# A two-layer hybrid decoder step: second chunk's input in its own stream, GpSimd's two-input work moved

## The chip, the cores and the metric

The kernel runs on one core of a Trainium2 chip. The core has TensorE (PE in the profile), VectorE (DVE), ScalarE (ACT), GpSimd (POOL) and SyncE (SP, here only an issuer of DMAs). The metric is the device time of one execution in microseconds, lower is better; the time of the kernel before is the median of three runs.

## The reference

One inference step of a two-layer decoder over 512 prompt tokens and 8 sample sequences of 8 new tokens each, model width 1024, all in float32. Per layer:

```
h = rmsnorm(x, norm_mix_g)
u, z, xbc, dt, cq, ckv, kpe = split(h @ w_in)            # 1702 columns
pool = windows 2/4/8/16 of u, minus u, times pool_w
ssd  = Mamba-2 scan over silu(causal conv4(xbc)), gated by silu(z), rmsnorm
mla  = 6 heads on a compressed latent: q = rmsnorm(cq) @ w_uq, rotary part,
       scores against rmsnorm(ckv) and rope(kpe), softmax, values, rmsnorm
x = x + concat(pool, ssd, mla) @ w_out
x = x + square(relu(rmsnorm(x) @ w_up)) @ w_down         # 4096 hidden
```

The sample sequences also read a paged cache of 1024 past positions (a page table picks the pages), and past pool, conv and scan states. After the layers comes one last rmsnorm; the new states, latents and rope keys are outputs too.

## The kernel before

Activations lie transposed: 128 features in the partitions, tokens along the free axis. The tokens are two chunks: chunk 0 is prompt tokens 0 to 255, chunk 1 is prompt tokens 256 to 511 and the 64 sample tokens (320 wide). Every matmul with big weights is done in three passes on rounded halves (`gemm`, L196): high weights by high activations, high by low, low by high (the lines L201 to L203 of the profile). `wblock` (L183) loads 128 x 512 pieces of a weight on the SP queue, rounds each on ScalarE (L191) and makes the low half by a subtraction (L192): on VectorE for w_up and w_down, and for w_in, w_out and w_uq on GpSimd for the first piece of a block and on VectorE for the second. A block of eight k tiles is 24 matmuls.

The work of one layer and chunk is a set of generators made by `mixer` (L348): `w_in` (14 blocks of the input projection, each evacuated by `evac`, L460), `mla_proj`, `prompt_attn`, `sample_attn` (chunk 1 alone), `ssd_dt`/`ssd`/`ssd_out`, `pool_out`, `mla_out` and `w_out`. They wait for each other by names (`need`, `mark`). `Weave` (L272) writes them down in turns: it always advances the generator whose sum of yielded costs, divided by its rate, is smallest; a generator that waits yields None. A scheduler then orders the instructions of each engine from that order of writing, with shifts of priority (`tc.high_priority`, `tc.cur_priority`). On an engine the instructions then run strictly in that order. Weights are written 100 steps ahead, evacuations of w_in 500, the scan and prompt attention 1000.

`start` (L328) loads the input of chunk 0 in eight pieces and prepares it with `prep0` (L238): for each of eight k tiles a scaled high half on ScalarE and a low half on VectorE (`scaled_split`, L234), and the squares for the first RMS norm. The odd tiles are squared on ScalarE and added up on VectorE, the even ones are squared and added on GpSimd (L247 to L251); `rstd_of` (L210) sums the two over the partitions by matmuls with ones. Then the same is written for chunk 1 (L340 to L345), with the priority counter moved 400 steps later for this part.

The first stage writes the mixer of layer 0, chunk 0, then w_out of chunk 0 at rate 1.0 beside the mixer of chunk 1, until w_out is done and the input projection of chunk 1 is written (L1089 to L1096). After it the feed-forward part of chunk 0 (`ffn`, L995) goes beside attention of chunk 1; 64 steps of 24 matmuls each. `late` (L999) names the step after which w_out of the next mixer may start: 40 beside chunk 0, 24 beside chunk 1. Layer 1 repeats this: the mixer of chunk 0 (its attention beside the feed-forward part of layer 0, chunk 1), then chunk 1.

A convolution tile (`conv_tile`, L387) is: product with rstd into XB on VectorE, copies of the halo on GpSimd (L391, L398), one tensor-scalar and three scalar-tensor-tensor steps on VectorE (L400, L402), a sigmoid of three ScalarE steps, and the gating product (L405, L407) on GpSimd. XB has one buffer. GpSimd also has the gate of z (L479), the rope residue of each cache piece (L671), the scaling of the probabilities (L581, L698), the windows of the pool (L436) and the scan state of the samples (L886, L890).

`prompt_attn` (L558) goes through three pairs of heads; for each head and each block of 128 queries: scores, row maximum (L576) and its negation (L577) on VectorE, exponential with its sum on ScalarE, reciprocal, scaling on GpSimd, transposes on PE, evacuation into pT (two buffers, a tag that the sample attention shares), and products with the values (L591) into one half of the partitions of `po`.

## Time and profile before

| what | value |
|---|---|
| median of 3 runs | 1501.34 us (1498.47 to 1504.32) |
| profiled execution | 1500.04 us |
| its span | 1498.2 us |
| PE busy | 1418.7 us (95%) |
| VectorE busy | 1067.8 us (71%) |
| ScalarE busy | 816.9 us (55%) |
| GpSimd busy | 341.5 us (23%) |
| granted TensorE clock, mean | 0.98 |

Busy times are sums over an engine's instructions in the one profiled execution. A busy PE is not PE at its peak, since matmuls overlap and their ends are modelled; the stages differ, so the table by stages among the rows below is read before the totals.

### The profile page before, as it was taken

Reading aid. Unit: us, or ns where it says so; the run is one execution under the profiler, and the core shown is the slowest. Engines: PE = TensorE matmul, PEld = TensorE weight load, DVE = VectorE, ACT = ScalarE, POOL = GpSimd, SP = SyncE. Lnnn points to the kernel's source line nnn. Section 1 sums busy time; section 2 is a strip of 40 time slices with the busy share of each in tenths; the row PEclk is TensorE's granted clock in tenths of the full one; section 3 lists DMA queues with packets and bytes.
Section 4 is the critical chain, followed back from the end, with each engine's and each line's share of the span. In section 5 each row is a group of like instructions: output and inputs, shape, how many; then the busy total and the mean of one; then the engine's idle time right before and its main releaser. Section 6 shows DMA issues by size and latency. Waiting matters only on the chain.

```text
span 1498.2 us, 30372 instructions
## 1 busy us (share of the span) xinstructions
PE 1418.7 (95%) x10528; PEld 1355.6 (90%) x10528; DVE 1067.8 (71%) x2225; ACT 816.9 (55%) x1717; POOL 341.5 (23%) x458
## 2 busy tenths in 40 slices
PE   5988988999999979999999999999999999999997
PEld 4867977998999978999999998889989999999997
DVE  7878759776666779865566668976866667765765
ACT  6555636555565656655454556545656565443444
POOL 5456424222200235200100035511231011000000
PEclk8999999999999999999999999989999999999999
DMA  6322425667546634434554543455675455444443
GB/s 215 108 96 77 146 70 172 201 201 211 154 138 186 199 106 135 149 104 149 163 153 153 168 153 111 149 169 165 197 225 158 135 174 165 152 150 149 149 152 108
DMA packets 151995, 228.96 MB, mean 153 GB/s; under 512 B 17826, under 2 KB 60962, under 8 KB 151714
## 3 DMA queue, kind: packets, MB, share of 16 engines
q1 hardware_dynamic: 138178, 216.69, 46.3%
q10 hardware_dynamic: 13664, 10.34, 2.3%
q8 instruction: 83, 1.36, 0.4%
q14 instruction: 70, 0.57, 0.1%
HBM read 219.32 MB, written 7.64 MB: 151 GB/s over the span
## 4 chain that ended last, share of the span: by engine, by line
PE 81%; DVE 11%; issue 2%; DMA 2%; ACT 2%; SPq 1%; POOL 0%; ACTq 0%; DVEq 0%; POOLq 0%
PE dn L203 9%; PE dn L201 9%; PE dn L202 9%; PE up L203 9%; PE up L201 9%; PE up L202 9%; PE in L203 2%; PE in L202 2%; PE in L201 2%; PE out L201 2%; PE out L202 2%; PE out L203 2%; PE o L591 2%; DVE cv L402 2%; PE spo L717 1%
## 5 line engine op out<-in xcount | busy, mean ns | idle before, releaser
L201 PE MATMUL up<-gh_f,wh_up 128*128 128x256 f32 (+1 forms) x1024 | 308.7, 302 | 5.0 <-DVE UE L425 2.6
L203 PE MATMUL up<-gh_f,wl_up 128*128 128x256 f32 (+1 forms) x1024 | 307.2, 301 | 3.4 <-DVE wl_up L192 1.9
L202 PE MATMUL up<-gl_f,wh_up 128*128 128x256 f32 (+1 forms) x1024 | 306.9, 300 | 0.7 <-DVE gl_f L236 0.5
L201 PE MATMUL dn<-hh,wh_dn 128*128 128x256 f32 (+1 forms) x1024 | 303.8, 297 | 3.3 <-ACT wh_dn L191 3.2
L203 PE MATMUL dn<-hh,wl_dn 128*128 128x256 f32 (+1 forms) x1024 | 304.2, 297 | 0.0
L202 PE MATMUL dn<-hl,wh_dn 128*128 128x256 f32 (+1 forms) x1024 | 303.3, 297 | 0.0
L191 ACT ACTIVATE wh_dn<-wr_dn 128x512 fp32r<-128x512 f32 x256 | 160.9, 631 | 184.6 <-PE dn L202 126.1
L191 ACT ACTIVATE wh_up<-wr_up 128x512 fp32r<-128x512 f32 x256 | 160.3, 630 | 172.4 <-PE up L202 107.4
L192 DVE TENSOR_TENSOR wl_dn<-wr_dn,wh_dn 128x512 fp32r<-128x512 f32 x256 | 179.2, 701 | 84.1 <-ACT wh_dn L191 72.6
L192 DVE TENSOR_TENSOR wl_up<-wr_up,wh_up 128x512 fp32r<-128x512 f32 x256 | 182.2, 715 | 73.6 <-ACT wh_up L191 63.3
L201 PEld LDWEIGHTS up<-gh_f,wh_up 128*128 128x128 f32 x1024 | 195.4, 191 | 9.0 <-DVE UE L425 2.8
L203 PEld LDWEIGHTS up<-gh_f,wl_up 128*128 128x128 f32 x1024 | 195.2, 191 | 6.8 <-DVE wl_up L192 4.6
L202 PEld LDWEIGHTS up<-gl_f,wh_up 128*128 128x128 f32 x1024 | 195.7, 191 | 2.6 <-DVE gl_f L236 0.8
L201 PEld LDWEIGHTS dn<-hh,wh_dn 128*128 128x128 f32 x1024 | 193.3, 189 | 3.9 <-ACT wh_dn L191 3.7
L203 PEld LDWEIGHTS dn<-hh,wl_dn 128*128 128x128 f32 x1024 | 193.2, 189 | 1.4 <-issue 0.7
L202 PEld LDWEIGHTS dn<-hl,wh_dn 128*128 128x128 f32 x1024 | 193.3, 189 | 1.2 <-issue 0.9
L201 PE MATMUL in<-gh_h,wh_in 128*128 128x256 f32 (+3 forms) x448 | 137.9, 308 | 16.2 <-DVE cq L490 7.5
L203 PE MATMUL in<-gh_h,wl_in 128*128 128x256 f32 (+3 forms) x448 | 137.6, 307 | 3.5 <-DVE wl_in L192 2.4
L202 PE MATMUL in<-gl_h,wh_in 128*128 128x256 f32 (+3 forms) x448 | 137.2, 306 | 2.1 <-DVE gl_h L236 2.1
L192 POOL TENSOR_TENSOR wl_in<-wr_in,wh_in 128x512 fp32r<-128x512 f32 (+1 forms) x55 | 72.9, 1326 | 155.8 <-ACT wh_in L191 149.8
L192 POOL TENSOR_TENSOR wl_out<-wr_out,wh_out 128x512 fp32r<-128x512 f32 x32 | 41.8, 1306 | 278.7 <-ACT wh_out L191 278.7
L201 PEld LDWEIGHTS in<-gh_h,wh_in 128*128 128x128 f32 (+1 forms) x448 | 85.1, 190 | 18.9 <-issue 7.9
(349 smaller groups left out, 2849.4 us busy)
## 6 DMA issues: line engine op xcount, KB each, us to landing
wr_up<-in_w_up SPq DMA_DIRECT2D x256, 256.0 KB, 2.8
wr_dn<-in_w_down SPq DMA_DIRECT2D x256, 256.0 KB, 2.8
wr_in<-in_w_in SPq DMA_DIRECT2D x110, 256.0 KB, 2.8
wr_out<-in_w_out SPq DMA_DIRECT2D x64, 256.0 KB, 2.9
ku<-in_kcache SPq DMA_DIRECT2D x96, 128.0 KB, 2.9
nat<-in_ncache SPq DMA_DIRECT2D x96, 64.0 KB, 2.0
ku<-in_kcache ACTq DMA_DIRECT2D x32, 128.0 KB, 3.7
wr_uq<-in_w_uq SPq DMA_DIRECT2D x12, 256.0 KB, 2.8
```

What stands on the lines that cost most here:

```text
L191: A.activation(hh, r, AF.Copy)
L192: (V if eng == 'v' or (f and eng is None) else G).tensor_tensor(ll, r, hh.bitcast(F32), op=ALU.subtract)
L201: T.matmul(ps[:mw, :cw], wh[:, kk, :mw], ah, start=(k == 0), stop=False)
L202: T.matmul(ps[:mw, :cw], wh[:, kk, :mw], al, start=False, stop=False)
L203: T.matmul(ps[:mw, :cw], wl[:, kk, :mw], ah, start=False, stop=(k == nk - 1))
L402: V.scalar_tensor_tensor(cv[:, :n], X[:, k:k + n], par(l, 'conv_w', m * 4 + k), cv[:, :n], op0=ALU.mult, op1=ALU.add)
L591: mark_pe[f"pa{l}{c}"] = T.matmul(po[64 * hh:64 * hh + 64, b * P:b * P + P], vT[i // 2][:, i % 2, h * 64:h * 64 + 64], pT[:, i * P:i * P + ...
L717: mark_pe[f"s{l}{2 * pq_ + 1}"] = T.matmul(po[:, 64 * u:64 * u + NR], nat[:, g], pT[:, o_:o_ + NR], start=False, stop=True, skip_group_che ...
```

## The change

- The chunk-1 input is no longer written in `start` but by a generator `prep1` in the weave, at rate 0.8, from the fourth block of w_in on; it loads in four pieces.
- `prep0` squares all eight tiles on ScalarE. For chunk 0 each square is added up by a matmul with ones as it comes; for chunk 1 the squares overwrite the input and `rstd_of` adds eight of them with matmuls.
- w_out of chunk 0 in layer 0 is written at rate 2.0; before it the weave runs until the chunk-1 input is prepared.
- `late` is 28 instead of 40 beside chunk 0.
- Gating products, rope residues and all low weight halves are on VectorE; the probabilities are scaled on ScalarE.
- In `prompt_attn` both heads of a pair are transposed before their value products, which alternate between the heads.
- The row maximum is negated in the reduction itself.

```
--- before.py
+++ after.py
@@ -90,7 +90,7 @@
 def step_kernel(ctx: ExitStack, tc: tile.TileContext, I, O):
     nc = tc.nc
     V, A, G, T, S = nc.vector, nc.scalar, nc.gpsimd, nc.tensor, nc.sync
-    E_XA, E_Z, E_KR, E_PR = G, G, G, G
+    E_XA, E_Z, E_KR = V, V, V
 
     const = ctx.enter_context(tc.tile_pool(name="const", bufs=1))
     wp = ctx.enter_context(tc.tile_pool(name="wp", bufs=2))
@@ -189,7 +189,7 @@
                 lo = wp.tile([P, HB, P], F32R, tag="wl", name=f"wl_{name}_{f}", bufs=NWL)
                 r, hh, ll = raw[:, :, :mw], h[:, :, :mw], lo[:, :, :mw]
                 A.activation(hh, r, AF.Copy)
-                (V if eng == 'v' or (f and eng is None) else G).tensor_tensor(ll, r, hh.bitcast(F32), op=ALU.subtract)
+                V.tensor_tensor(ll, r, hh.bitcast(F32), op=ALU.subtract)
                 halves.append((h, lo))
         return halves
 
@@ -207,11 +207,14 @@
 
     mark_pe = {}
 
+    ps0 = [None]
+
     def rstd_of(c, ssum, n, name, tag):
         cw = CW[c]
-        ps = psum("tp", f"ss_{name}")
+        ready, ps0[0] = ps0[0], None
+        ps = ready if ready is not None else psum("tp", f"ss_{name}")
         parts = ssum if isinstance(ssum, list) else [ssum]
-        for i, t in enumerate(parts):
+        for i, t in enumerate(parts if ready is None else ()):
             mark_pe[name] = T.matmul(ps[:, :cw], ones, t, start=(i == 0), stop=(i == len(parts) - 1)).ins
         r = ap.tile([P, CM], F32, tag=tag, name=f"r_{name}", bufs=2)[:, :cw]
         A.activation(r, ps[:, :cw], AF.Ln, bias=eps, scale=1.0 / n)
@@ -235,21 +238,23 @@
         A.activation(hl[0][:, k], src, AF.Copy, scale=g)
         V.scalar_tensor_tensor(hl[1][:, k], src, g, hl[0][:, k].bitcast(F32), op0=ALU.mult, op1=ALU.subtract)
 
-    def prep0(c, tile_k, pool_sum, sq_tile, home=None):
+    def prep0(c, x, home):
         hl = act_tiles(c, f"h0_{c}")
-        acc = ssum_tile(c, f"h0_{c}")
+        sq = []
         for k in range(KT):
-            t = tile_k(k)
-            scaled_split(t, hl, k, par(0, 'mix_g', k))
-            if k % 2:
-                sq_acc(c, acc, t, k == 1, f"h0_{c}{k}", home)
-            elif k == 0:
-                G.tensor_tensor(pool_sum, t, t, op=ALU.mult)
+            scaled_split(x[:, k, :CW[c]], hl, k, par(0, 'mix_g', k))
+            if c:
+                t = x[:, k, :CW[c]]
             else:
-                q = sq_tile(k)
-                G.tensor_tensor(q, t, t, op=ALU.mult)
-                G.tensor_tensor(pool_sum, pool_sum, q, op=ALU.add)
-        h_in[c], ss_in[c] = hl, [acc, pool_sum]
+                t = home.tile([P, CM], F32, tag="sq", name=f"sq_h0_{c}{k}", bufs=3)[:, :CW[c]]
+            A.activation(t, x[:, k, :CW[c]], AF.Square)
+            sq.append(t)
+            if c == 0:
+                if k == 0:
+                    ps0[0] = psum("tp", "ss_h00")
+                T.matmul(ps0[0][:, :CW[c]], ones, t, start=(k == 0), stop=(k == KT - 1))
+            yield 2.0
+        h_in[c], ss_in[c] = hl, sq
 
     def norm_prep(c, xm, acc, hl, k, g, name):
         sq_acc(c, acc, xm, k == 0, f"{name}{k}")
@@ -333,17 +338,18 @@
             S.dma_start(x0[:, k, :CW[0]], I['x0'][:, k])
         first[0] = tc.cur_priority
         load_consts(mp)
-        part = ep.tile([P, 2, CM], F32, name="part")
-        scr = ep.tile([P, 2, CM], F32, name="scr")
-        prep0(0, lambda k: x0[:, k, :CW[0]], part[:, 0, :CW[0]], lambda k: scr[:, k // 2 % 2, :CW[0]])
+        for _ in prep0(0, x0, ep):
+            pass
         x_res[0] = x0
-        at = tc.cur_priority
-        tc.cur_priority = at + 400
+        G.memset(Ez, 0.0)
+
+    def prep1(ep):
+        while not done_of[0, 0].issuperset(('cq1', 'ckv')):
+            yield None
         x1 = ep.tile([P, KT, CM], F32, name="x1_in")
-        S.dma_start(x1, I['x1'])
-        prep0(1, lambda k: x1[:, k], part[:, 1], lambda k: scr[:, k // 2 % 2], ep)
-        tc.cur_priority = at
-        G.memset(Ez, 0.0)
+        for k in range(0, KT, 2):
+            S.dma_start(x1[:, k:k + 2], I['x1'][:, k:k + 2])
+        yield from prep0(1, x1, ep)
 
     def mixer(l, c, mp, ep):
 
@@ -559,11 +565,12 @@
             qT, o = st['qT'], st['o']
             for j in range(3):
                 po = psum('ac', f"o{l}{c}{j}")
-                for hh in range(2):
-                    h = 2 * j + hh
-                    for b in range(2):
-                        nb = 2 * c + b + 1
-                        nk = nb * P
+                for b in range(2):
+                    nb = 2 * c + b + 1
+                    nk = nb * P
+                    pTs = []
+                    for hh in range(2):
+                        h = 2 * j + hh
                         q = qT[:, h, b * P:b * P + P]
                         sc = psum("sc", f"sc{l}{c}{h}{b}")
                         if c == 1:
@@ -573,25 +580,28 @@
                             T.matmul(sc[:, :nk], q, kT[0][:, h, :nk], start=True, stop=True)
                         T.matmul(sc[:, nk - P:nk], idb, matt, start=False, stop=True, skip_group_check=True)
                         nm = mp.tile([P, 4], F32, tag="nm", name=f"nm{l}{c}{h}{b}", bufs=3)
-                        V.tensor_reduce(nm[:, 0:1], sc[:, :nk], axis=AX.X, op=ALU.max)
-                        V.tensor_scalar(nm[:, 1:2], nm[:, 0:1], -1.0, None, op0=ALU.mult)
+                        V.tensor_reduce(nm[:, 1:2], sc[:, :nk], axis=AX.X, op=ALU.max, negate=True)
                         pr = mp.tile([P, 512], F32, tag="pr", name=f"pr{l}{c}{h}{b}", bufs=NPR)
                         A.activation(pr[:, :nk], sc[:, :nk], AF.Exp, bias=nm[:, 1:2], accum_out=nm[:, 2:3])
                         V.reciprocal(nm[:, 3:4], nm[:, 2:3])
-                        E_PR.tensor_scalar(pr[:, :nk], pr[:, :nk], nm[:, 3:4], 1.0, op0=ALU.mult, op1=ALU.mult)
+                        A.activation(pr[:, :nk], pr[:, :nk], AF.Copy, scale=nm[:, 3:4])
                         tp = psum("tp", f"pt{l}{c}{h}{b}")
                         for i in range(nb):
                             T.transpose(tp[:, i * P:i * P + P], pr[:, i * P:i * P + P], idn)
                         pT = mp.tile([P, 512], F32, tag="pT", name=f"pT{l}{c}{h}{b}", bufs=NPT)
-                        if b:
+                        if hh:
                             A.activation(pT[:, :nk], tp[:, :nk], AF.Copy)
                         else:
                             V.tensor_copy(pT[:, :nk], tp[:, :nk])
-                        for i in range(nb):
+                        pTs.append(pT)
+                        yield 0.4 * nb
+                    for i in range(nb):
+                        for hh in range(2):
+                            h = 2 * j + hh
                             mark_pe[f"pa{l}{c}"] = T.matmul(
                                 po[64 * hh:64 * hh + 64, b * P:b * P + P], vT[i // 2][:, i % 2, h * 64:h * 64 + 64],
-                                pT[:, i * P:i * P + P], start=(i == 0), stop=(i == nb - 1)).ins
-                        yield 0.55 * nb
+                                pTs[hh][:, i * P:i * P + P], start=(i == 0), stop=(i == nb - 1)).ins
+                    yield 0.3 * nb
                 A.activation(o[:, j, :CP], po[:, :CP], AF.Copy)
 
         def sample_attn():
@@ -650,8 +660,7 @@
                 pair_q(pq_)
 
                 def unit(i, sc, pr):
-                    V.tensor_reduce(nm[:, i:i + 1], sc, axis=AX.X, op=ALU.max)
-                    V.tensor_scalar(nm[:, 3 + i:4 + i], nm[:, i:i + 1], -1.0, None, op0=ALU.mult)
+                    V.tensor_reduce(nm[:, 3 + i:4 + i], sc, axis=AX.X, op=ALU.max, negate=True)
                     A.activation(pr, sc, AF.Exp, bias=nm[:, 3 + i:4 + i], accum_out=nm[:, 6 + i:7 + i])
                     prs.append(pr)
 
@@ -695,7 +704,7 @@
                 prn, prs = prs[1], (prs[0], prs[2])
                 V.tensor_scalar(prn, prn, nm[:, 2:3], None, op0=ALU.mult)
                 V.tensor_scalar(prs[0], prs[0], nm[:, 0:1], None, op0=ALU.mult)
-                G.tensor_scalar(prs[1], prs[1], nm[:, 1:2], 1.0, op0=ALU.mult, op1=ALU.mult)
+                A.activation(prs[1], prs[1], AF.Copy, scale=nm[:, 1:2])
                 po = psum('sp', f"spo{l}{c}{pq_}")
                 tp = psum("tp", f"sptn{l}{c}{pq_}")
                 T.transpose(tp[:CS, :P], prn, idn)
@@ -996,7 +1005,7 @@
         cw = CW[c]
         x = x_res[c]
         hid = {}
-        late, late_of = (40, 24)[c], beside
+        late, late_of = (28, 24)[c], beside
 
         def up(g, j):
             w = wblock(I['w_up'][l, g * GT + j], f"up{l}{c}{g}{j}", eng='v')
@@ -1080,6 +1089,7 @@
             W.add(M['mla'], 0.5, 500)
             W.add(M['ssd'], 0.8, 1000)
             if l == 0 and c == 0:
+                W.add(prep1(ep), 0.8)
                 done_of[l, c].add('go')
             W.add(M['attn'], 0.3, 1000)
             W.add(M['smp'], 0.5, 500)
@@ -1091,7 +1101,8 @@
             if l == 0:
                 start(mp, fp)
                 m0 = proj(0, 0, fp)
-                W.add(m0['w_out'], 1.0)
+                W.run(lambda: h_in[1] is not None)
+                W.add(m0['w_out'], 2.0)
                 m1 = proj(0, 1, fp)
                 W.run(lambda: 'wo' in done_of[0, 0])
             else:
```

## Rows read from the trace of the kernel before

**Rows 1.** The page: engine totals, and the chain that ended last by engine.
```profile
PE 1418.7 (95%) x10528; PEld 1355.6 (90%) x10528; DVE 1067.8 (71%) x2225; ACT 816.9 (55%) x1717; POOL 341.5 (23%) x458
...
PE 81%; DVE 11%; issue 2%; DMA 2%; ACT 2%; SPq 1%; POOL 0%; ACTq 0%; DVEq 0%; POOLq 0%
```

**Rows 2.** Table by stages: busy us of PE, PEld, DVE, ACT, POOL; granted clock; DMA.
```profile
0.00:275.00 275.00, 232.04 (x1686) 207.15 (x1687) 211.50 (x485) 156.27 (x370) 130.87 (x191) 0.94 0.42 133
...
25.00:50.00 25.00, 12.84 (x87) 12.25 (x87) 17.77 (x47) 14.24 (x33) 10.92 (x12) 0.73 0.26 91
...
525.00:625.00 100.00, 87.70 (x653) 82.72 (x653) 83.89 (x187) 60.98 (x138) 40.41 (x55) 0.97 0.39 121
...
625.00:875.00 250.00, 250.00 (x1734) 245.63 (x1733) 159.60 (x309) 134.37 (x271) 19.52 (x26) 1.00 0.49 154
```

**Rows 3.** Waits of PE, all stages: us in total, times, longest.
```profile
PE q L201 <- DVE qT L531: 13.9, 2, 12.2
...
PE in L201 <- DVE cq L490: 7.5, 1, 7.5
```

**Rows 4.** Chain of waits, 14 to 44 us: start, us, what.
```profile
14.65 0.99 PE ss_in L215 x4
...
26.18 0.12 PE q L201
...
29.36 1.14 DVE gl_h L236
...
39.24 0.21 PE q L202
```

**Rows 5.** Timeline, 0 to 20 us, ScalarE and PE.
```profile
9.28 0.42 ACT L226 ACTIVATE sq_h<-x_in 128x256 f32<-128x256 f32 x1 [0.85 <-DVE ssum_h L227]
...
9.61 0.89 ACT L235 ACTIVATE gh_h<-x_in,prm 128x256 fp32r<-128x256 f32 x2
...
15.05 0.59 PE L215 MATMUL ss_in<-part,ones 128*128 128x256 f32 x2
```

**Rows 6.** Groups by form, VectorE, 0 to 275 us: busy us, mean ns, idle before.
```profile
L236 DVE SCALAR_TENSOR_TENSOR gl_h<-x_in,prm,gh_h 128x320 fp32r<-128x320 f32 x8 | 6.2, 786 | 0.0
...
L954 DVE SCALAR_TENSOR_TENSOR fn<-x_in,prm,r_f 128x256 f32<-128x256 f32 x8 | 5.7, 746 | 0.0
```

**Rows 7.** Groups by form, whole span, GpSimd and VectorE.
```profile
L192 POOL TENSOR_TENSOR wl_in<-wr_in,wh_in 128x512 fp32r<-128x512 f32 x51 | 69.3, 1359 | 149.7 <-ACT wh_in L191 143.6 <-DVE cq L490 2.3 <-DVE ah L807 2.1
...
L405 POOL TENSOR_TENSOR xaz<-cv,se 128x256 f32<-128x256 f32 x20 | 17.4, 870 | 17.3 <-ACT se L415 15.7 <-PE in L202 1.6
...
L192 DVE TENSOR_TENSOR wl_dn<-wr_dn,wh_dn 128x512 fp32r<-128x512 f32 x256 | 179.2, 701 | 84.1 <-ACT wh_dn L191 72.6 <-PE dn L203 2.3 <-ACT o L730 2.3
...
L402 DVE SCALAR_TENSOR_TENSOR cv<-XB,prm,cv 128x344 f32<-128x344 f32 x30 | 24.3, 809 | 0.6
...
L1035 DVE TENSOR_TENSOR x<-x,dn 128x256 f32<-128x256 f32 x32 | 13.3, 417 | 6.4 <-PE dn L203 6.2
```

**Rows 8.** Timeline, 118 to 142 us, VectorE and GpSimd.
```profile
119.36 0.57 DVE L402 SCALAR_TENSOR_TENSOR cv<-XB,prm,cv 128x344 f32<-128x344 f32 x1
...
123.17 3.08 DVE L402 SCALAR_TENSOR_TENSOR cv<-XB,prm,cv 128x344 f32<-128x344 f32 x3
...
123.25 1.65 POOL L192 TENSOR_TENSOR wl_in<-wr_in,wh_in 128x512 fp32r<-128x512 f32 x1 [0.36 <-ACT wh_in L191]
...
138.14 1.77 POOL L391 COPY XB<-halo 128x3 f32<-128x3 f32 x1 [1.69 <-DVE cv L402]
```

**Rows 9.** Chain of waits, 80 to 90 and 420 to 432 us.
```profile
86.12 0.69 PE y L871 x9
...
424.17 0.80 PE o L591 x6
...
428.66 1.02 PE o L591 x8
...
429.67 0.32 PE up L202
```

## The prediction

> **What bounds the kernel now.** I read the engine totals and the chain of waits first. PE is busy 95% of the span and 81% of the chain is PE, but 11% of the chain, some 165 us, is DVE [rows 1]. The table by stages then says where. From 625 to 875 us PE has no idle time at all; from 0 to 275 us it is idle for 43 us and works through 1686 matmuls where the saturated stage does 1734 in 250 us, and from 525 to 625 us it is idle for 12 us [rows 2]. In these two stages, the projections with convolution, scan and attention around them, VectorE is busy 77 and 84% and GpSimd 48 and 40%; so they are set by VectorE's order and latency, and PE only fills in. The waits of PE hold two large single ones: 12.2 us on the first queries and 7.5 us on the first block of layer 1 [rows 3]. The change touches mostly the first stage; the feed-forward stages can lose only what PE itself has less to do.
>
> The profiled execution took 1500.04 us for a span of 1498.2 us; the median of the runs is 1501.34, so a sum made against the one holds for the other within 1.3 us.
>
> **The second chunk's input in its own stream.** Before, its scaling, splitting and squaring stand before the first mixer in the order of writing, with 400 steps of delay; they land at 27 to 40 us, where PE's in-order queue waits for the query's evacuation behind them. In the chain of that stretch gl_h instructions of up to 1.14 us alternate with tiny ones, and after the pause the matmuls come every 0.21 us, not 0.12 as before it [rows 4], at the lower of the two clock levels (0.73 is the mean granted over 25 to 50 us [rows 2]); I count 18 of them until the step falls back, so 18 x 0.09 = 1.6 us. In the new code the stream starts after the fourth block and takes one of 8 steps per 2.0/0.8 = 2.5 units, 20 units in all, while the remaining ten blocks take 10 x 2.67 = 27; so it is through before the second chunk's mixer is written, and the added run-until is no wait of its own. The pause and the slow matmuls go: -13.8. What comes back: the 8 split instructions of VectorE, 6.2 us with their stalls, about 4.5 without [rows 6], now beside the convolutions, of which a third is on the chain there: +1.5. Eight matmuls with ones instead of two give the sum: 4 passes took 0.99 us for 256 columns [rows 4], 0.31 for 320 by width, so 12 passes more are +3.7, all at one point where the second mixer opens. Four SP issues instead of one, behind the weights, cost nothing as long as SP runs ahead. Sum -8.6; bounds -14 and +3 (the stall only moves, below).
>
> **The first chunk's input.** GpSimd's multiply-adds go, ScalarE does eight squares instead of four, and PE adds each as it comes. Before, the last part of the sum ran on PE from 15.05 us for 0.59. ScalarE's new list (eight casts at 0.89 a pair, eight squares at 0.42 [rows 5]) is 6.9 us from about 4.5, with two weight casts between, so the last square ends near 12.5 and the sum near 13.2: -2, bounds 0 and -3. The extra passes fall into PE's wait for gl_h.
>
> **GpSimd's two-input work to VectorE.** Moved are 99 weight halves (51 and 4 short in w_in, 32 in w_out, 12 in w_uq) at 0.70 us, the price of the same form where GpSimd is silent; 64 rope residues and 32 gates at 0.42, the price of two 256-wide inputs, plus 10 small ones: 69 + 42 = 111 us more on VectorE, 1068 to about 1180 of 1498 before relief [rows 1, 7]. On GpSimd a half took 1.36 and a gate 0.87 [rows 7]. Against it stands what GpSimd takes from VectorE: a scalar-tensor-tensor instruction of 344 elements took 0.57 us alone, and three took 3.08 while a weight half ran on GpSimd [rows 8]; the mean of 30 is 0.81 [rows 7]. Over 60 such instructions that is about 15 us, and the fp32 splits, window means and norms of the first stage (gl_h 0.79, fn 0.75 where 0.55 and 0.48 would do) [rows 6] bring it to some 40 us in the first stage by the same reckoning, an estimate. So in the mixers VectorE gets 69 us (47 of halves in w_in and w_uq, 16 of gates, 6 of w_out) and loses perhaps 60 to 70: I take nothing for its load, and -3 for GpSimd leaving the path between a convolution and the next (a three-column copy took 1.77 us there [rows 8]). Bounds: +36 and -17 (rivals). The rope residues lie beside feed-forward matmuls, where VectorE has a third of its time free.
>
> The Trainium skill (SBUF — State Buffer, Who interferes with whom) says that a VectorE instruction with two SBUF inputs and a GpSimd instruction that reads SBUF shut each other out for a whole instruction, whoever starts first. Rows 8 agree in both directions. The rule also speaks against the change: the copies that stay on GpSimd meet more such VectorE work than before.
>
> **Prompt attention.** Both heads of a pair now finish their transposes before their value products, which run head by head in turn. A group of 8 passes took 1.02 us and one of 6 took 0.80, so 0.11 a pass and 0.14 for the group, and the next feed-forward matmul 0.32 [rows 9] instead of 0.12. Merging two groups saves 0.34. There are 48 groups in four mixers; 36 of them lie beside feed-forward matmuls, where PE binds, and become 18: -6. The scan's product, which already alternates halves, took 0.69 for 9 passes, 0.077 each [rows 9]; at that price 200 passes would save 6.6 more; I take -5 in all: the merging nearly whole and nothing of the alternation, since a transpose buffer is now held longer and the two there are shared with the sample attention. Bounds 0 and -13. Negation inside the maximum, and probabilities scaled on ScalarE (57% busy in the first stage [rows 2]) instead of GpSimd, lie beside PE work and are costed at nothing; if ScalarE were late, attention would trail feed-forward work that is there anyway.
>
> **w_out sooner.** Rate 2.0 turns the eight blocks of the first chunk from 26.4 units into 13.2; attention still ends before, so they start where they did and end some four input blocks sooner. PE's work is only reordered, but the norm for the feed-forward part (fn 5.7 us and its residues [rows 6]) leaves the crowded end at 225 to 250 us: -4, bounds +2 and -7. The release at step 28 instead of 40 changes nothing: a step is 3.0/2.0 = 1.5 units, so step 40 is 60 units in, while the second chunk's attention needs 3 x 7.7 = 23.1 at rate 0.3, 77 units. The output projection waits for attention either way, and the 7.5 us pause [rows 3] stays, less 2 for unhindered norms.
>
> **Sum:** -8.6 - 2 - 3 - 5 - 4 - 2 = -24.6, from 1500 to about 1476.
>
> **Rivals.** (A) The forecast, 1476, own range 1467 to 1487. (B) VectorE's relief is larger than its load and the mixers shrink as well: the stalls that go pay for the load in each of the 20 convolution tiles, and where GpSimd's results came last the half and the gate come 0.66 and 0.45 us sooner [rows 7], 1.11 a tile; in three of four mixers, 15 tiles, that is 17: 1459. For it: GpSimd's queue holds weights, gates and copies in one order. Against: VectorE is near full there already. (C) The pause moves: the second chunk's first block waits for its prepared input, because ScalarE and VectorE do it last among everything in 40 to 95 us; the 13.8 come back with the added 3.7 already counted: 1490, or 1495 with attention's gain lost too. (D) Slower: VectorE becomes the bound of the convolution tiles. Place: 20 tiles; price: 1.2 us each for half and gate, 24, and the remaining copies at 1.0 instead of 0.4 by the worst row [rows 8], 12; with what the other steps bring (-19) 1517. It decides from the point where VectorE has no gap between tiles; in the first stage it has 63 us of gaps [rows 2], which speaks against.
>
> **How the numbers follow.** Chances: A 0.47, B 0.22, C 0.18, D 0.13. About 0.5%, 7.5 us, is what a measurement of this kernel can tell from no change. Faster by more than that (below 1494): A, B and a third of C, 0.75; within it: most of C and the edge of D, 0.13; slower 0.12. The range 1456 to 1500 leaves out half of B's lower side and D, about 0.2.
>
> **What would show it.** Right: no idle time of PE over 4 us between 20 and 45 us; the second prepared input between 30 and 95 us; weight halves at 0.70 us on VectorE and a 344-wide convolution step near 0.6; GpSimd under 120 us; products of attention in groups of 12 and 16 passes; w_out of the second chunk starting near the same feed-forward step as before. Wrong: VectorE busy over 95% from 100 to 200 us with the convolution on the chain throughout, a PE pause where the second chunk's projection starts, or first feed-forward matmuls that come no sooner than before.

## The result, and the profile after

The changed kernel takes 1456.21 us (median, 1453.98 to 1457.84) against 1499.9 (1498.11 to 1504.32): ratio 0.9703, interval 0.9677 to 0.973. That is 44 us, where 25 were forecast. The profiled execution took 1453.98 us for a span of 1452.2. Measured once more beside e13, e14 and e16 (e15 below), the same kernel took 1459.02, ratio 0.974 (0.9715 to 0.9765): 39 us.

The page after: engine totals, and the chain that ended last by engine. They answer to [rows 1].
```profile
PE 1405.4 (97%) x10552; PEld 1344.1 (93%) x10552; DVE 1063.3 (73%) x2353; ACT 843.6 (58%) x1781; POOL 74.7 (5%) x182
...
PE 89%; DVE 5%; DMA 2%; ACT 2%; issue 1%; SPq 0%; ACTq 0%; DVEq 0%
```
The span fell by 46.0 us. PE's busy time fell by 13.3 (1418.7 to 1405.4) and its idle time by 32.7, from 79.5 to 46.8 (span less busy). VectorE's share of the chain went from 11 to 5%, although its busy time stayed: 1067.8 before, 1063.3 after, with 128 instructions more. GpSimd gave up 267 us of work; some 223 of it (halves, rope residues, gates) went to VectorE, the scalings to ScalarE. Summed over the form groups, VectorE took over 206 instructions (107 us as they run there) and lost 78 (72 negations and 6 sums of squares, 18 us). Its total did not rise because the instructions that both kernels have became some 90 us shorter. That is the line to remember for what follows.

The table by stages after (busy us of PE, PEld, DVE, ACT, POOL; granted clock; DMA), which answers to [rows 2].
```profile
0.00:275.00 275.00, 249.05 (x1820) 222.85 (x1821) 218.24 (x564) 171.95 (x412) 33.71 (x95) 0.96 0.44 142
25.00:50.00 25.00, 21.32 (x148) 20.45 (x149) 21.00 (x66) 16.34 (x38) 1.30 (x6) 0.86 0.43 142
525.00:625.00 100.00, 98.67 (x718) 91.40 (x717) 84.83 (x216) 67.86 (x167) 8.62 (x23) 0.98 0.40 130
625.00:875.00 250.00, 249.99 (x1726) 245.86 (x1725) 165.16 (x321) 132.19 (x253) 2.34 (x8) 1.00 0.48 153
```
In the first 275 us PE gets through 1820 matmuls instead of 1686; the saturated stretch is what it was.

The waits of PE after (us in total, times, longest), which answer to [rows 3].
```profile
PE in L201 <- DVE cq L496: 7.9, 1, 7.9
PE in L201 <- ACT gh_h L238: 5.0, 1, 5.0
PE in L201 <- ACT se L419: 3.4, 1, 3.4
PE cb L869 <- ACT bt L848: 3.2, 2, 2.1
PE q L201 <- DVE qT L537: 1.8, 1, 1.8
```
The query's 12.2 us are 1.8; layer 1's pause of 7.5 us is 7.9.

Where the time went, from stage to stage by the first matmul of each stage in PE's timeline (us; the run names are those of the next section):

| stretch | before | after | e1 | e7 | e4 | e17 |
|---|---|---|---|---|---|---|
| layer-0 mixers, to the first up | 233.9 | 225.2 | 229.1 | 225.1 | 238.2 | 237.0 |
| first chunk's feed-forward, attention beside it | 298.6 | 284.6 | 295.0 | 292.7 | 291.9 | 292.5 |
| layer 1, first chunk's mixer | 71.7 | 66.1 | 65.8 | 66.8 | 71.8 | 76.0 |
| second chunk's feed-forward | 267.8 | 271.1 | 271.1 | 269.7 | 268.3 | 271.9 |
| layer 1, second chunk's mixer | 74.4 | 65.7 | 65.8 | 69.8 | 74.4 | 73.1 |
| the rest of layer 1 | 551.8 | 539.5 | 544.7 | 548.1 | 541.9 | 541.4 |

The two small mixer stretches repeat within 1 us where the code is the same; the large ones vary by some 4 us from one execution to the next (the last is 547.5 in e3, which changes nothing in it). The forecast saw most of its gain in the first row. It gave 8.7; the two stages with attention beside feed-forward work gave 14.0 and 12.3, and layer 1's mixers 14.3, of which 3.3 came back in the stage between them.

Form groups of VectorE after (busy us, mean ns, idle before), which answer to [rows 6, 7].
```profile
L192 DVE TENSOR_TENSOR wl_in<-wr_in,wh_in 128x512 fp32r<-128x512 f32 x102 | 70.0, 686 | 8.3 <-ACT wh_in L191 6.7
...
L408 DVE SCALAR_TENSOR_TENSOR cv<-XB,prm,cv 128x344 f32<-128x344 f32 x30 | 17.2, 572 | 0.4
...
L408 DVE SCALAR_TENSOR_TENSOR cv<-XB,prm,cv 128x256 f32<-128x256 f32 x30 | 14.3, 477 | 0.2
...
L239 DVE SCALAR_TENSOR_TENSOR gl_h<-x_in,prm,gh_h 128x320 fp32r<-128x320 f32 x8 | 4.1, 543 | 1.6 <-ACT gh_h L238 1.5
...
L963 DVE SCALAR_TENSOR_TENSOR fn<-x_in,prm,r_f 128x256 f32<-128x256 f32 x8 | 3.6, 476 | 0.6 <-ACT r_f L221 0.6
```
The last four now have the duration that only their undisturbed instances had before: 0.57 for the 344-wide step (mean 0.81 before), 0.48 for the 256-wide one (0.74), 0.54 for gl_h (0.79), 0.48 for fn (0.75).

The chain of waits after, 410 to 440 us (start, us, what), which answers to [rows 9].
```profile
412.42 0.72 PE o L601 x12
...
414.21 0.31 PE up L202
...
417.35 1.02 PE o L601 x14
```
A group of 6 took 0.80 us before and one of 12 takes 0.72; one of 8 took 1.02 and 14 take as long.

### The profile page after: what moved, and what is told of

The parts are those of the page before. It is cut to its first block, busy times and chain, and to the rows that moved or that the text cites. A ratio compares the mean times of both kernels' runs of the same rounds, so it can differ in the third digit from the quotient of the medians.

```text
span 1452.2 us, 30116 instructions
## 1 busy us (share of the span) xinstructions
PE 1405.4 (97%) x10552; PEld 1344.1 (93%) x10552; DVE 1063.3 (73%) x2353; ACT 843.6 (58%) x1781; POOL 74.7 (5%) x182
## 3 DMA queue, kind: packets, MB, share of 16 engines
q1 hardware_dynamic: 138610, 216.69, 46.8%
## 4 chain that ended last, share of the span: by engine, by line
PE 89%; DVE 5%; DMA 2%; ACT 2%; issue 1%; SPq 0%; ACTq 0%; DVEq 0%
PE dn L203 9%; PE dn L201 9%; PE dn L202 9%; PE up L203 9%; PE up L202 9%; PE up L201 9%; PE in L201 4%; PE in L203 4%; PE in L202 4%; PE out L201 2%; PE out L203 2%; PE out L202 2%; PE spo L726 2%; PE o L601 2%; PE rb L856 1%
## 5 line engine op out<-in xcount | busy, mean ns | idle before, releaser
L201 PE MATMUL up<-gh_f,wh_up 128*128 128x256 f32 (+1 forms) x1024 | 305.4, 299 | 1.8 <-ACT gh_f L238 1.1
L192 DVE TENSOR_TENSOR wl_up<-wr_up,wh_up 128x512 fp32r<-128x512 f32 x256 | 177.6, 696 | 63.1 <-ACT wh_up L191 55.3
L191 ACT ACTIVATE wh_in<-wr_in 128x512 fp32r<-128x512 f32 (+1 forms) x110 | 67.3, 614 | 61.3 <-PE in L202 49.5
L203 PEld LDWEIGHTS in<-gh_h,wl_in 128*128 128x128 f32 (+1 forms) x448 | 84.8, 189 | 4.0 <-DVE wl_in L192 2.2
```

What stands on the lines that cost most here:

```text
L191: A.activation(hh, r, AF.Copy)
L192: V.tensor_tensor(ll, r, hh.bitcast(F32), op=ALU.subtract)
L201: T.matmul(ps[:mw, :cw], wh[:, kk, :mw], ah, start=(k == 0), stop=False)
L203: T.matmul(ps[:mw, :cw], wl[:, kk, :mw], ah, start=False, stop=(k == nk - 1))
```

## The experiments

Each run is compared with runs of the kernel before on the same chip; the ratios carry the comparison, with their 95% intervals.

| run | what it is | median us | ratio |
|---|---|---|---|
| e1 | before + moves from GpSimd | 1475.21 | 0.9865 (0.9846 to 0.9884) |
| e2 | after, moves undone | 1484.03 | 0.9919 (0.99 to 0.9939) |
| e3 | before + input stream, squares by matmul | 1498.11 | 1.001 (0.9997 to 1.0023) |
| e4 | before + order of prompt attention | 1488.4 | 0.995 (0.9933 to 0.9968) |
| e5 | before + w_out's two numbers | 1497.67 | 1.0001 (0.9984 to 1.0019) |
| e6 | before + rope residue moved | 1492.67 | 0.9965 (0.9948 to 0.9982) |
| e7 | before + weight halves moved | 1476.59 | 0.9864 (0.9838 to 0.989) |
| e8 | before + gates moved | 1490.13 | 0.9948 (0.9929 to 0.9967) |
| e9 | after, input as before | 1465.48 | 0.9787 (0.9762 to 0.9811) |
| e10 | before + moves + input stream | 1470.45 | 0.9817 (0.979 to 0.9844) |
| e11, e16 | after, fn in other buffers | 1454.98, 1458.03 | 0.972 (0.9696 to 0.9743), 0.9733 (0.9707 to 0.9759) |
| e12 | e4 without alternation | 1494.95 | 0.9972 (0.9954 to 0.999) |
| e13 | after, w_out's numbers as before | 1463.13 | 0.9758 (0.9734 to 0.9783) |
| e14 | after, attention's order as before | 1469.03 | 0.9811 (0.9787 to 0.9835) |
| e15 | after again | 1459.02 | 0.974 (0.9715 to 0.9765) |
| e17 | after, GpSimd halves twice | 1496.17 | 1.0001 (0.9986 to 1.0017) |

**The four parts (e1 to e4).** e1 and e2 make and undo this:
```diff
-    E_XA, E_Z, E_KR, E_PR = G, G, G, G
+    E_XA, E_Z, E_KR, E_PR = V, V, V, G
...
-                (V if eng == 'v' or (f and eng is None) else G).tensor_tensor(ll, r, ...)
+                V.tensor_tensor(ll, r, ...)
...
-                        E_PR.tensor_scalar(pr[:, :nk], ...)
+                        A.activation(pr[:, :nk], ...)
...
-                G.tensor_scalar(prs[1], ...)
+                A.activation(prs[1], ...)
```
e3 takes over `prep0`, `prep1` and `rstd_of` with their calls, e4 the loops of `prompt_attn`.

> The kernel before with only GpSimd's two-input work moved: gates, rope residues and all low weight halves on VectorE, probabilities scaled on ScalarE. Theory M (the moves carry most of the gain, in all four mixers and beside both attention stages): about 1473 us, -27; the stretch from the first w_in matmul of layer 1 to its first up matmul falls from 71.7 to about 66 us, and the one of chunk 1 from 74.3 to about 66. Theory P (as predicted: the load on VectorE and the relief cancel, -3): about 1497 us, with the two stretches as before. The 12.2 us pause of PE at 26 us stays by both, perhaps shortened to 9 by M.

> The changed kernel with GpSimd's two-input work put back where it was (gates, rope residues, first weight halves, probabilities); the input stream, attention order, earlier w_out and negated maxima stay. Theory M: about 1482 us, -18 against before. Theory P: about 1459, as the whole change less 3.

> The kernel before with only the input part: squares summed by matmuls for both chunks, the second chunk's input in its own stream, w_out's rate as before. Theory P: -10.6 us, about 1489, with no PE pause over 4 us between 20 and 45 us. Rival S (the first stage is set by VectorE's total work, so a pause removed comes back at the second chunk's projection): within 4 us of before.

> The kernel before with only the order of prompt attention changed (both heads transposed, value products in turn between the heads); scaling of the probabilities stays on GpSimd and the maximum is negated by its own instruction. Predicted: -5 us, about 1495. Theory H (passes that alternate between halves of the columns also go faster, 0.08 instead of 0.11 us): -8 to -13. Rival B (the two shared transpose buffers hold attention up): no gain, or slower by up to 5.

The moves alone give 20 us (1.35%), and the changed kernel loses about 27 without them (0.9919 against 0.974 for e15). The attention order gives 7.5. The negated maxima (72 VectorE instructions, 10.5 us of its busy time) stand in no run alone. The input stream alone gives nothing, and its trace says in part why. PE's waits in e3, 0 to 60 us:
```profile
PE q L201 <- DVE qT L537: 5.6, 1, 5.6
PE in L201 <- ACT gh_h L238: 4.9, 1, 4.9
PE q L201 <- DVE XB L396: 1.1, 1, 1.1
```
The pause shrinks from 12.2 to 5.6 us only. It is not that GpSimd still lengthens the splits. They take 0.55 us in e3 as well, with GpSimd's halves in place (and 0.70 in e9, with the halves moved but GpSimd's squares back, so it was the squares that lengthened them):
```profile
L239 DVE SCALAR_TENSOR_TENSOR gl_h<-x_in,prm,gh_h 128x320 fp32r<-128x320 f32 x8 | 4.3, 546 | 0.6 <-ACT gh_h L238 0.6
```
But they come late. SyncE issues the loads of the second chunk's input at 30.24 us in e3, all four; in the changed kernel the first two go out at 15.67:
```profile
30.24 1.91 SPq L351 DMA_DIRECT2D x_in<-in_x  x4
```
```profile
15.67 0.90 SPq L351 DMA_DIRECT2D x_in<-in_x  x2
```
So the splits (33.8 to 39.8 us) again stand before the last evacuations of the query. The loads are late (30 to 31 us) also in e2 and e17, where GpSimd subtracts too, and at 15.67 in e10, where it doesn't; why SyncE's order follows that was not taken apart. PE idles 9 us less in the first stage, and 5 us of passes with ones and 2 us of matmuls at the slower cadence come back in it (summed over PE's timeline).

**Which of the moves (e6 to e8, e5 beside them).** Each makes one of the moves of the diff above: e6 `E_KR` alone, e7 the halves alone, e8 `E_XA` and `E_Z`. e5 has
```diff
-        late, late_of = (40, 24)[c], beside
+        late, late_of = (28, 24)[c], beside
...
-                W.add(m0['w_out'], 1.0)
+                W.add(m0['w_out'], 2.0)
```

> Kernel before with the two numbers of the order of writing alone: the late point of the first chunk at step 28 instead of 40, and the first chunk's output weights written at rate 2.0 instead of 1.0. Theory W (the prediction's step): the output projection of the first chunk gets out of the first stage's tail and saves about 4 us: 1492 us. Rival N: in the kernel before the projection's steps are released by what they wait for, not by their place in the order; 1496 us, within 2 us of before, and the first output matmul of the first chunk stays near 140 us. Rival S: sooner output weights take ScalarE and the DMA queue from the input projection: 1500 us.

> Kernel before with the residue of the cached rope rows (kh, 64 of 0.89 us on GpSimd) alone moved to VectorE. Theory K: the page buffers come free sooner and the queue of loads is no longer held behind the pages; that is what the moves gave in the two stages of first-chunk feed-forward (3.6 and 7.1 us with all moves made): 1486 us. Rival H: those gains came from the weight halves and the gates, which share the port with VectorE; the rope residue alone gives under 2 us: 1495 us. Theory K has it that the layer-1 mixer stretches (first mixer matmul of layer 1 to the first up matmul) stay at 72 and 74 us.

> Kernel before with the low weight halves alone moved from GpSimd to VectorE (1.3 us each on GpSimd, 0.70 on VectorE). Theory H: VectorE's own work runs faster once GpSimd is quiet (conversion steps 0.74 and 0.81 us towards 0.48 and 0.57) and low halves are sooner there; the two layer-1 mixer stretches lose most of the 5.9 and 8.5 us that all moves gave, the first stage 3: 1481 us. Rival G: the gates and the XB copy left on GpSimd keep the convolution slow, and VectorE has 19 us more to do: 1494 us. Rival L: the load on VectorE decides and it is slower: 1500 us.

> Kernel before with the x gates and z gates alone moved from GpSimd to VectorE (0.87 us and less on GpSimd). Theory C (contention is what the moves take away, whoever's instruction it is): conversion steps on VectorE fall part of the way (0.74 and 0.81 us towards 0.65 and 0.72) and the layer-1 mixer stretches lose 2 to 3 us each: 1491 us. Rival H (only the weight halves matter, because PE waits for them and for nothing behind the gates): 1497 us, within 2 us of before.

The halves alone give all 20 us of the moves; the gates alone 8, the rope residue alone 5. The rope residue lies between its two theories. The three add up to more than the moves together give, so what they take away overlaps. What it is, the page's engine totals of e7, its chain by engine and two of its form groups on VectorE begin to show:
```profile
PE 1414.4 (96%) x10528; PEld 1350.7 (92%) x10528; DVE 1071.8 (73%) x2325; ACT 816.9 (55%) x1717; POOL 216.5 (15%) x358
...
PE 86%; DVE 6%; DMA 3%; ACT 2%; issue 2%; SPq 1%; ACTq 0%; DVEq 0%; POOL 0%; POOLq 0%
```
```profile
L402 DVE SCALAR_TENSOR_TENSOR cv<-XB,prm,cv 128x344 f32<-128x344 f32 x30 | 19.3, 643 | 0.4
L402 DVE SCALAR_TENSOR_TENSOR cv<-XB,prm,cv 128x256 f32<-128x256 f32 x30 | 16.9, 564 | 0.4
```
VectorE took on a hundred instructions of up to 0.70 us, some 68 us, and its busy time rose by 4. The other 64 were paid back by shorter instructions elsewhere, the convolution steps among them (0.81 to 0.64, 0.74 to 0.56). On the chain, VectorE falls from 11 to 6% by this edit alone. The pause on the queries goes with it, which no expectation had (e1's had it stay). PE's waits in e7 from 14 to 60 us:
```profile
PE in L201 <- ACT wh_in L191: 5.1, 1, 5.1
PE in L203 <- DVE wl_in L192: 2.1, 1, 2.1
PE q L201 <- ACT wh_uq L191: 0.2, 1, 0.2
```
That is 7.4 us instead of 12.2 (7.7 in e1), with the second chunk's input prepared as before; with the gates or the rope residue alone it stays above 12. e5 is inert, as its second theory had it.

**The same subtraction twice (e17).** A half on VectorE is also ready sooner. To tell that from the relief, e17 keeps the halves on VectorE and lets GpSimd do the old work once more for nobody:
```diff
                 V.tensor_tensor(ll, r, hh.bitcast(F32), op=ALU.subtract)
+                if not (eng == 'v' or f):
+                    G.tensor_tensor(r, r, hh.bitcast(F32), op=ALU.subtract)
```

> Kernel after, in which GpSimd does the subtraction of the weight halves that it did before once more, into the raw tile that nobody reads any more (95 of about 1.36 us); the halves that PE uses still come from VectorE. Theory C (GpSimd's two-input work beside VectorE is the cost): conversion steps go back from 0.57 to near 0.75 us for 344 elements, layer-1 mixer stretches back to 70 us and more, the kernel takes 20 us more than after: 1476 us. Theory L (the cost was that the halves came late, 1.36 us behind everything in GpSimd's queue): within 4 us of after, 1456 to 1460 us. A raw tile comes free later in this kernel, as it did before; PE would show it as a wait for weights.

All of the gain goes: ratio 1.0001. Engine totals of e17, then GpSimd's added groups, then its chain of waits by engine:
```profile
PE 1418.3 (95%) x10552; PEld 1354.4 (91%) x10552; DVE 1128.0 (76%) x2353; ACT 845.6 (57%) x1781; POOL 220.1 (15%) x282
```
```profile
L194 POOL TENSOR_TENSOR wr_in<-wr_in,wh_in 128x512 f32<-128x512 f32 x51 | 77.9, 1528 | 202.4 <-DVE wl_in L192 186.7 <-issue 6.7 <-DVE sm L797 3.1
L194 POOL TENSOR_TENSOR wr_out<-wr_out,wh_out 128x512 f32<-128x512 f32 x32 | 45.3, 1417 | 662.4 <-DVE wl_out L192 437.7 <-DMA wr_up<-in_w_up 204.3 <-DMA wr_dn<-in_w_down 15.5
L194 POOL TENSOR_TENSOR wr_uq<-wr_uq,wh_uq 128x512 f32<-128x512 f32 x12 | 17.2, 1438 | 28.6 <-issue 17.4 <-DVE wl_uq L192 7.6 <-DVE sm L792 1.5
```
```profile
PE 78%; DVE 12%; issue 3%; DMA 2%; ACT 2%; SPq 0%; POOL 0%; DVEq 0%; ACTq 0%; POOLq 0%
```
VectorE executes the same 2353 instructions as in the changed kernel and needs 64.7 us more for them (1128.0 against 1063.3), while GpSimd is busy 145 us longer (220.1 against 74.7). There are 100 subtractions (282 instructions against 182; four short ones and the first piece are not shown), so each costs VectorE about 0.65 us, nearly as much as doing the half itself (0.69). The Trainium skill (SBUF — State Buffer, Who interferes with whom) says that a VectorE instruction with two SBUF inputs and a GpSimd instruction that reads SBUF exclude each other; the trace agrees as far as VectorE's list is lengthened, and 0.65 us is the price here. The time was missed all the same: 1476 expected, 1496 measured. VectorE here bears both its own halves and the stretch, and the raw tiles come free later, behind GpSimd. On the chain VectorE goes from 5 to 12% and "issue" from 1 to 3%; whether the tiles stand behind the latter is not shown. Late halves can't be most of it: PE's own waits for low weight halves add up to 6.1 us before, 2.3 after and 4.7 in e17. How much of the 40 us is stretch and how much the tiles, or GpSimd's other work behind the added subtractions, stays open.

**Does the input stream ever pay (e9, e10)?** e9 puts `prep0`, `start` and `rstd_of` of the kernel before back into the changed one; e10 is e1 and e3 together.

> Kernel after with the preparation of both chunks' input put back as before (second chunk's input in the first stage's start, squares on VectorE and GpSimd); moves, attention order, output weights and negated maxima stay. Theory I (interaction: alone the stream gave nothing because GpSimd's halves kept the first stage slow, with the moves it gives): 1464 us, 8 over the kernel after, and the pause of the query matmuls near 40 us is back. Rival Z: the preparation gives nothing here either, and the moves and the attention order make up the whole: 1457 us. Rival B (the stream costs): 1452 us.

> Kernel before with the moves from GpSimd and the preparation of the input together; attention order, output weights and negated maxima as before. Theory I (the preparation gives only where GpSimd is quiet): moves 20, preparation 9 as the kernel after loses without it: 1469 us. Rival A (the preparation's 9 us need the attention order, not the moves): 1477 us, the time of the moves alone.

In place it pays: the changed kernel loses 7 to 13 us without it (0.9787 against 0.974 and 0.9703), and its first stage is 236.8 us instead of 225.2 (227.4 in e15). On top of the moves alone it gives about 7 by the ratios (0.9817 against 0.9865, intervals just apart), but the profiled spans differ by 2.7 only, and PE's waits from 14 to 60 us by 1.5 (7.7 in e1, 6.2 in e10). That the stream needs the moves is therefore likely; that it also needs the attention order or the output weights is not excluded. e9 missed one thing that its first theory had: the pause on the queries is not back. PE waits there 5.1 us for wh_in and 2.5 for wl_in, as in e1 and e7, since the halves alone had taken that pause away.

**Attention's order (e12, e14).** e12 keeps e4's merged groups and takes the alternation out; e14 puts the loops of before back into the changed kernel.
```diff
-                    for i in range(nb):
-                        for hh in range(2):
+                    for hh in range(2):
+                        for i in range(nb):
                             h = 2 * j + hh
```

> Kernel before with the prompt attention's order of the changed kernel (groups of both heads merged), but the products of one head issued after those of the other instead of in turn. Theory P (the prediction's: merging two groups into one saves, alternation nothing): as the run with the attention order alone, 1488 to 1491 us, and the o products in each stretch of first-chunk feed-forward stay near 6.9 us. Rival T (two products that write different halves of the rows of one bank run beside each other when they alternate, and that is what saves): o products 9 to 10 us a stretch, 1494 us.

> Kernel after with the prompt attention's order as before: groups per head, query block inside, no alternation; the rest stays. Theory A2 (the attention order carries what e10 lacks to the kernel after): 1468 to 1470 us. Rival A1 (it is worth here what it is worth alone): 1463 to 1464 us.

PE's group of these products in before, e12 and e4:
```profile
L591 PE MATMUL o<-pT,vT 128*64 128x128 f32 x240 | 35.3, 283 | 1.5 <-ACT pT L587 1.5
```
```profile
L596 PE MATMUL o<-pT,vT 128*64 128x128 f32 x240 | 33.3, 283 | 1.7 <-DVE pT L590 1.7
```
```profile
L596 PE MATMUL o<-pT,vT 128*64 128x128 f32 x240 | 26.9, 285 | 1.3 <-DVE pT L590 1.3
```
In e12's chain 12 passes of one head after the other took longer than 12 alternating ones in the changed kernel (0.72, above):
```profile
294.46 1.07 PE o L596 x12
```
By the ratios merging gives 4.2 us of e4's 7.5 and alternation 3.3, with intervals that overlap, so in the time alternation's share is likely, not shown. Of PE's busy time on these products merging takes 2.0 us and alternation 6.4, which is shown. Counted from each start to the next in PE's timeline, a stretch of first-chunk feed-forward spends 10.9 us on them before, 9.0 in e12 and 6.9 in the changed kernel. Theory T holds for the products (9.0 us a stretch, 1494.95 us); the prediction's "nothing of the alternation" is wrong for PE's work. The Trainium skill (TensorEngine Tiling (Array Packing), Key Properties) says that narrower tiles of the array work independently; the products here have 64 columns each, and alternating heads write different halves, and the trace agrees (26.9 us alternating, 33.3 not). In the changed kernel the order is worth 10 us (1469.0 against 1459.0, e15).

**The rest (e13, e15, e11, e16).** e13 undoes e5's two lines in the changed kernel; e15 is the changed kernel again on the same chip.

> Kernel after with the late point back at step 40 and the first chunk's output weights back at rate 1.0. Theory W2 (with the moves made, the sooner output weights matter): 1461 us, 5 over the kernel after. Rival N (they are inert here as in the kernel before): 1456 us, within 2 us of after.

> The kernel after again, to stand on the same chip and in the same rounds as the other three: 1456 us.

1463.1 against 1459.0, with intervals that overlap: four us for the sooner output weights are likely, not shown.

e11, and e16 again beside e15, take the normalised rows out of the pool that closes at the end of layer 0:
```diff
-                pl, w_, tag, bufs = (ep, cw, "fn", 3) if c == 0 else (tr[0], 512, "ku", NK)
+                pl, w_, tag, bufs = (ep, cw, "fn", 3) if c == 0 else (mp, 512, "pr", NPR)
```

> Kernel after with one buffer changed: the normalised rows of the second chunk before its first-layer feed-forward (fn) lie in the two buffers of the attention probabilities instead of the page buffers of the pool that closes there. Theory S (the pause of 7.9 us at the start of layer 1 is a wait for space: cq of the next pool lies where fn lay, so all eight fn must be done first): cq comes after the second fn, the pause falls to 2 us or less: 1450 us. Rival Q (cq waits for its factor r_in and for VectorE's queue, not for space): 1456 us. Rival F: the later fn delays the feed-forward's first matmuls, 1456 to 1460 us.

> The kernel after with the normalised rows in the buffers of the attention probabilities, again, beside the kernel after. Theory S2 (the pause that went is worth its place: stretch to the first mixer matmul's end 2.2 us, pause 7.9 us of which slow matmuls and a 2.0 us wait come back): 1452 to 1453 us. Rival R (given back later): 1455 to 1456 us.

VectorE's timeline in e11 at the start of layer 1 (in the changed kernel cq came at 524.04, behind all eight fn):
```profile
514.27 1.01 DVE L963 SCALAR_TENSOR_TENSOR fn<-x,prm,r_f 128x320 f32<-128x320 f32 x2 [1.04 <-ACT r_f L221]
515.21 0.75 DVE L496 TENSOR_TENSOR cq<-in,r_in 128x256 f32<-128x256 f32 x2
```
So the pause was a wait for space: in the changed kernel cq is released by the last gl_f, of which it reads nothing, and with fn in another place it passes six of the eight. (The new place has two buffers, the old one three, so fn is spread out as well.) PE's wait for cq falls from 7.9 to 0.9 us. The time doesn't follow: other waits appear behind it (2.0 on sm, 1.2 on ckvn), and e16 stands at 1458.0 beside 1459.0. No version tried beats the changed kernel by more than its runs vary.

## Why the prediction was wrong in size

**The step that failed** is "I take nothing for its load, and -3 for GpSimd leaving the path". The moves are worth 20 us alone and about 27 in place. The working below it was nearly right: the load was put at 111 us (99 halves; there are 100) and measured 107, the relief at 60 to 70 in the mixers and is some 90 in all, and VectorE's total stayed (1067.8 and 1063.3). What failed is the inference that load and relief which cancel in VectorE's total cancel in time. The instructions that became shorter were ones that PE waited for: with the halves alone (e7) VectorE is busy 4 us longer and its share of the chain falls from 11 to 6%. That the added halves fell where VectorE had gaps is a reading of this, not shown by itself.

**Rival B** (1459) has the number, 3 us from the median, and half of the mechanism. Its first half, that the relief outweighs the load, is what the runs show in time (e7, e17), though not in VectorE's busy total, and in e7 the mixer stretches give 18 us where B had 17. But B priced those 17 by halves and gates that come 1.11 us a tile sooner, and nothing bears that out: e1 with the gates is no faster than e7 without, and e17 keeps the sooner halves and loses all. More than half of the gain also came beside attention, where B saw none beyond the forecast's. So its number is in part luck. Its argument against, VectorE nearly full, does not hold: from 100 to 200 us VectorE is busy 76.6 us before and 77.6 after. Rival D's point, no gap between tiles, is never reached; e17 is near its load and costs what before cost.

**The input stream**, forecast at -8.6, gave nothing alone and 7 to 13 in place. Its largest term, 13.8 for the pause and the slow matmuls, was not its own: the halves alone take the pause from 12.2 to 7.4 us (e7), and the stream alone to 7.1 (5.6 the longest wait), since its loads went out late (e3). That the splits' stalls would go was right: 0.55 us in e3 already. The second input was prepared from 21.8 us on, sooner than the 30 that was given. The eight matmuls with ones were priced at +3.7; the group before took 1.59 us on the chain and the one after, 14 of its 16 passes, 3.97:
```profile
100.72 3.97 PE ss_in L218 x14
```
That is at least +2.4. The first chunk's sum ends at 14.2 us instead of 15.6: -1.4 of the -2.

**Attention**, forecast at -5, gave 7.5 alone and 10 in place: merging was put too high (6 against 4.2 or less) and alternation too low (0 against 3.3 or more). **w_out**, forecast at -4: 0 alone, perhaps 4 in place. That step 28 releases nothing sooner held nearly: the second chunk's first output matmul comes 51 us ahead of layer 1 before (481.8 to 532.5) and in e13, and 54 after. **The pause of layer 1** was to lose 2 us to faster norms. The norms did get faster (0.54 us), but VectorE's stretch from the first of them to cq fell only from 8.6 to 7.9 us, and PE's pause in it grew from 7.5 to 7.9.

Of the list of what would show it, the idle time (longest 1.8 us between 20 and 45), the half (0.69), the convolution step (0.57), GpSimd's total (74.7) and the groups of 12 and 14 or more passes came as said.

The parts alone add up to 20 + 7.5 + 0 + 0 = 27.5 us, the whole gives 39 to 44. The difference lies in the input stream, the attention order and perhaps w_out, each worth more in place than alone, and in what the negated maxima give, which no run shows; why the attention order gains 2 to 3 us more there was not taken apart.

## What to carry to other kernels

Work that GpSimd does beside VectorE, both with two inputs from SBUF, is not free on VectorE: here a GpSimd half cost VectorE 0.65 us, where doing it itself takes 0.69. So compare VectorE's busy total with and without, and look for forms whose mean is well above their shortest instance; an unchanged total can still be a large gain when the stretched instructions are those on the chain. Two edits can also aim at the same pause without looking alike: here the halves took most of what the input stream was to give. So look after each edit alone at the wait that another one is meant to remove, and try an edit that gives nothing again on top of the others.

## What the runs showed of the hardware

A hundred GpSimd subtractions, 145 us of its time, lengthened VectorE's unchanged list of 2353 instructions by 64.7 us. Two value products with 64 columns each that write different halves run beside each other when they alternate: 14 passes took 1.02 us, which 8 took before (240 passes: 26.9 us alternating, 33.3 not). A wait for the space of a tile of a pool that closes looks in the profile like a wait for an engine: PE's 7.9 us stood under VectorE's cq, which itself waited for the space of fn.
